# The last pair of row tiles gets an order of its own: column halves in two banks, residual and norm weights early, row factors on two engines

## The chip, the cores and the metric

The kernel runs on one core of one Trainium2 chip. The time is device microseconds (us) of that core for one execution of the whole program. Of the kernel before, three runs are shown: 2419.07, 2419.09 and 2419.3 us, so the median is 2419.09 us. A profiled execution of the same program took 2419.82 us. Times inside a profile are counted from the start of its span.

## The reference

A layer of a bidirectional encoder in float32, for a prompt of 2048 rows and a sample of 256 rows with 1024 columns each: a mixer half (Fourier mixing and retention) and an MLP half, both with a norm and a residual, and a last norm behind it. Only the end of the layer matters here:

```python
h = modulate(rmsnorm(x, norm_mlp), sh2, sc2)
x = x + gt2[:, None, :] * (jnp.square(jax.nn.relu(h @ w_mlp_in)) @ w_mlp_out)
return rmsnorm(x, norm_final)     # x * rsqrt(mean(x * x, -1) + EPS) * norm_final
```

So every output row needs its product with `w_mlp_out` (4096 x 1024), times the gate `gt2`, plus the residual `x`, and then one factor per row (the inverse root of its mean square) and one weight per column (`norm_final`).

## The kernel before, in words

The 2304 rows stand in 18 tiles of 128 rows. The last stage, from `HB = ...` on, multiplies the squared activations by `w_mlp_out`. It takes the tiles in nine pairs: pairs 0 to 7 are the prompt, pair 8 (tiles 16 and 17) is the sample. The inner dimension is cut into four rounds (`for r in range(NG)`), each with its own weights in SBUF. In the rounds 0 to 2 the partial sums of a pair go to HBM (`accd`) and come back in the round after; in the round 3 they are finished and stored.

A pair in a round is one 2 x 2 block product: two tiles of rows, two halves of the inner dimension, two halves of 512 columns. It is done with seven products in place of eight (`STEPS`, Winograd's form); I call them product 0 to product 6. A product multiplies a left operand (`A11`, `S2`, ..., from the tile `hr`) by a right operand (`B11`, `T2`, ..., held as `wo...`). Both are held as a high and a low part, so a product is three passes (high by high, high by low, low by high) over four slices of the inner dimension: 12 matmuls with 512 columns that add up in one PSUM bank. The left operand is the one loaded as weights; ScalarE (ACT) rounds it to its high part (a CAST at L80) and VectorE (DVE) subtracts to get the low part (L81), into a tile `ho`.

The products 0, 2, 4 and 6 share the bank X: product 2 is added on top of what product 0 left there, and so on. Products 3 and 5 share Z, product 1 has Y. After every product DVE adds the bank to one of the four blocks of the accumulator `acc` (L1201; `ADDR` gives the block: 0, 0, 1, 3, 3, 1, 2). Blocks 0 and 1 are the column halves of the pair's first tile, 2 and 3 those of the second. Product 2 may write X only when DVE has read what product 0 left, and so on up to product 6.

In round 3 a tile is done after product 5 (first tile) or product 6 (second). `finish_tile` (L1134 to L1138) handles 1024 columns at once: DVE multiplies by the gate and adds the residual `x1`, ACT squares and sums the row (L145), GpSimd (POOL) scales, adds EPS (L102) and raises to -0.5 (L105), DVE multiplies by the row factor `rr` and the norm weights `nf` (L1137), and SyncE (SP) issues the store. For the last pair `finish_block` (L1143 to L1146) does gate, residual and square by blocks of 512 columns, as soon as a block is whole, and `finish_rows` (L1148 to L1155) adds the two sums (DVE), forms the factor (POOL) and scales and stores both halves (DVE, SP).

The gate of the sample differs from that of the prompt. It is loaded just ahead of pair 8 (L888) into a slot of the pool `rawb`, where it has to wait until the gate of the prompt has had its last reader, L1134 of tile 15. The residual tiles `x1` rotate through the five slots of the pool `raw`.

The program is written in the order of the loops. A scheduler then sets the order on each engine, and every engine works through its own queue in that order. SP's queue holds all the loads and stores of the stage, so a load that waits there holds up those behind it.

Of the kernel before, what the change touches and what calls it, by code (L numbers as in the profile page):

```python
# [15 lines left out]
P = 128  # L16
# [15 lines left out]
def encoder(ctx: ExitStack, tc: tile.TileContext, a):  # L32
# [1110 lines left out]
    def finish_block(b, y, x1, ss):  # L1143
        dve.tensor_tensor(out=y, in0=y, in1=gate[:, halves(b)], op=ALU.mult)
        dve.tensor_tensor(out=y, in0=y, in1=x1[:, halves(b)], op=ALU.add)
        act.activation(x1[:, halves(b)], y, AF.Square, accum_out=ss[:, b % 2:b % 2 + 1])  # L1146

    def finish_rows(t, y, ss):  # L1148
        dve.tensor_tensor(out=ss[:, 2:3], in0=ss[:, 0:1], in1=ss[:, 1:2], op=ALU.add)
        r = rstd_from(ss[:, 2:3], 1, 1.0 / D)  # L1150
        for b in range(2):
            yb = y[:, 512 * b:512 * b + 512]
            dve.scalar_tensor_tensor(out=yb, in0=yb, scalar=r[:, 0:1], in1=nf[:, halves(b)],
                                     op0=ALU.mult, op1=ALU.mult)
            sp.dma_start(out=xrows("y", t)[:, halves(b)], in_=yb)  # L1155

    for r in range(NG):
        w = load_mo(r)
        if r == NG - 1:
            gate = load_gate(1, 0, lambda s: v1(s, "rawb"))  # L1160
            nf = v1("nf", "rawb")
            sp.dma_start(out=nf, in_=a["norm_final"].rearrange("(o c) -> o c", o=1).to_broadcast([P, D]))
        for pr in range(NT // 2):
            if r == NG - 1 and pr == NP // 2:
                gate = load_gate(1, 1, lambda s: v1(s, "rawb"))
            c, pc = divmod(pr, NPC)
            hv = v1("hr", f"hr{pr % 2}").rearrange("p (j b s) -> p j b s", j=GJ, b=7)
            sp.dma_start(out=hv[:, :, 0:NB[r], :].rearrange("p j b s -> p j (b s)"),
# [12 lines left out]
            if r == NG - 1:  # L1181
                x1 = [v1("x1", "raw") for _ in range(2)]
                for i in range(2):
                    sp.dma_start(out=x1[i], in_=x1d[2 * pr + i])
            at = {}
            ss = [tsm([P, 4], "ss") for _ in range(2)] if end else None
            for i, (ln, rn, bn) in enumerate(STEPS):
                ho = v1("ho", f"ho{nho[0] // 3 % 2}", F32R)
                nho[0] += 1
                hh, hl = ho[:, 0:512], ho[:, 512:1024]  # L1190
                split(src[ln], hh.rearrange("p (j s) -> p j s", j=GJ), hl.rearrange("p (j s) -> p j s", j=GJ))
                if i in (0, 1, 3):
                    at[bn] = bank(bn)
                o = at[bn]
                three(lambda p_, j, first, last: add_mm(
                    i, o, (hh, hh, hl)[p_][:, j * P:(j + 1) * P], w[j][rn][p_ % 2], first, last), range(GJ))
                b_ = ADDR[i]
                if r == 0 and i in (0, 2, 3, 6):
                    act.copy(acc[:, b_], o)
                else:  # L1200
                    dve.tensor_tensor(out=acc[:, b_], in0=o, in1=acc[:, b_], op=ALU.add)  # L1201
                if end:
                    if i not in (0, 2, 3):
                        finish_block(b_, acc[:, b_], x1[b_ // 2], ss[b_ // 2])
                    if i > 4:
                        finish_rows(2 * pr + b_ // 2, rows[b_ // 2], ss[b_ // 2])
                elif r == NG - 1 and i > 4:
# [78 lines left out]
```

## Time and profile before

| | |
|---|---|
| median of three runs | 2419.09 us |
| profiled execution, the run / its span | 2419.82 / 2417.9 us |
| PE (TensorE matmul) busy | 2349.4 us, 97% of the span, 11985 matmuls |
| DVE / ACT / POOL busy | 1465.5 / 1004.8 / 112.0 us |
| mean granted TensorE clock | 0.989 of full speed |
| product 6 of pair 8, the last one | starts at 2405.89 us, 12 matmuls, 3.00 us |
| last store issued | 2414.7 us |

Reading it: a row of the timeline has the start in us, the busy time in us, the engine, the line of the kernel, the operation, the tile written and the tile read, the shape and the count; in square brackets stands how long the engine had been idle before and what released it. Rows of one line that follow each other are merged. A row of the waits names who waited for whom, the total, the number of times and the longest. SPq is SyncE's queue, which issues DMAs. In the table of stages each row has the length of the stage, the busy time of PE, the weight loads (PEld), DVE, ACT and POOL, the granted clock and the DMA share.

### The profile page before, as it was taken

What the parts mean: (1) busy time and instruction counts of PE and PEld (TensorE: products, weight loads), DVE (VectorE), ACT (ScalarE), POOL (GpSimd) and SP (SyncE); (2) the same over time, 40 slices, a digit from 0 to 9 for tenths busy, and PEclk for the clock granted to TensorE, in tenths of its full rate; (3) what the DMA queues carried; (4) which work ended last, traced back from release to release, by engine and by line L of the source; (5) the groups of instructions that cost most, each with busy time, mean ns of one, the idle gap of its engine ahead of it and who ended that gap; (6) DMA issues with size and microseconds to landing.
All of it is one profiled execution on the core that took longest, in us unless ns stands there. A gap on an engine that the chain in (4) does not pass through costs nothing.

```text
span 2417.9 us, 30874 instructions
## 1 busy us (share of the span) xinstructions
PE 2349.4 (97%) x11985; PEld 2040.2 (84%) x11985; DVE 1465.5 (61%) x2188; ACT 1004.8 (42%) x1684; POOL 112.0 (5%) x191
## 2 busy tenths in 40 slices
PE   7999999999999999999999999999899999999998
PEld 4777787788887888999999999998688788787886
DVE  3574544334544754655685578556646867857788
ACT  4742222123333533555565566555334323224332
POOL 0101000001111000000000000000000000000000
PEclk9999999999999999999999999999899999999999
DMA  7547649323333455543453345443534645545774
GB/s 284 210 154 270 208 152 330 136 75 134 126 101 107 157 166 170 182 136 122 159 186 122 122 159 183 130 134 124 180 118 140 217 157 192 192 157 221 269 265 163
DMA packets 183770, 411.61 MB, mean 170 GB/s; under 512 B 12052, under 2 KB 80436, under 8 KB 176712
## 3 DMA queue, kind: packets, MB, share of 16 engines
q1 hardware_dynamic: 182040, 405.58, 48.7%
q0 software_dynamic: 1584, 4.06, 0.6%
q8 instruction: 94, 1.54, 0.3%
q14 instruction: 52, 0.43, 0.1%
HBM read 274.05 MB, written 135.54 MB: 169 GB/s over the span
## 4 chain that ended last, share of the span: by engine, by line
PE 82%; issue 8%; DVE 5%; DMA 2%; ACT 2%; POOL 1%; SPq 0%; POOLq 0%; DVEq 0%; ACTq 0%
PE mX L968 30%; PE proj L84 21%; PE mZ L968 15%; PE mY L968 7%; PE o L84 2%; PE ada L84 1%; PE dft L84 1%; PE tr L750 1%; DVE woT L81 1%; PE kvf L84 1%; DVE woB L81 1%; PE sc L84 1%; PE kvb L84 1%; POOL rr L105 1%; DVE acc L1201 1%
## 5 line engine op out<-in xcount | busy, mean ns | idle before, releaser
L968 PE MATMUL mX<-woT,ho 128*128 128x512 f32 x1296 | 312.3, 390 | 3.8 <-ACT x L1146 1.5
L80 ACT CAST ho<-hr 128x512 fp32r<-128x512 f32 x252 | 153.0, 621 | 345.3 <-PE mX L968 213.9
L968 PEld LDWEIGHTS mX<-woT,ho 128*128 128x128 f32 x1296 | 243.8, 188 | 56.5 <-issue 1.9
L968 PE MATMUL mX<-opS,wT 128*128 128x384 f32 x1152 | 208.0, 334 | 0.0
L84 PE MATMUL proj<-whi,hhi 128*128 128x512 f32 x720 | 192.0, 404 | 13.4 <-ACT hhi L80 7.8
L968 PEld LDWEIGHTS mX<-opS,wT 128*128 128x128 f32 x1152 | 200.4, 188 | 0.0
L81 DVE TENSOR_TENSOR ho<-hr,ho 128x512 fp32r<-128x512 f32 x252 | 170.2, 686 | 35.8 <-ACT ho L80 35.5
L84 PE MATMUL proj<-wlo,hhi 128*128 128x512 f32 x720 | 187.1, 397 | 0.0
L84 PE MATMUL proj<-whi,hlo 128*128 128x512 f32 x720 | 182.6, 392 | 0.0
L84 PEld LDWEIGHTS proj<-whi,hhi 128*128 128x128 f32 x720 | 132.2, 190 | 52.6 <-issue 10.9
L84 PEld LDWEIGHTS proj<-wlo,hhi 128*128 128x128 f32 x720 | 135.9, 191 | 32.3 <-issue 4.2
L84 PEld LDWEIGHTS proj<-whi,hlo 128*128 128x128 f32 x720 | 134.0, 188 | 30.5 <-issue 3.4
L81 DVE TENSOR_TENSOR wB<-mr,wB 128x1024 fp32r<-128x1024 f32 x72 | 87.9, 1221 | 81.6 <-ACT wB L80 81.4
L968 PE MATMUL mY<-woB,ho 128*128 128x512 f32 x432 | 112.0, 396 | 10.7 <-ACT woB L80 7.2
L1201 DVE TENSOR_TENSOR acc<-mX,acc 128x512 f32<-128x512 f32 x117 | 79.9, 687 | 65.5 <-PE mX L968 59.0
L968 PE MATMUL mX<-woB,ho 128*128 128x512 f32 x432 | 111.8, 398 | 6.0 <-ACT ho L80 5.9
L968 PE MATMUL mZ<-woT,ho 128*128 128x512 f32 x432 | 109.7, 395 | 5.9 <-ACT woT L80 5.5
L968 PE MATMUL mY<-opA,wB 128*128 128x384 f32 x576 | 106.1, 338 | 2.4 <-DVE x L159 2.4
L968 PEld LDWEIGHTS mY<-woB,ho 128*128 128x128 f32 x432 | 81.8, 191 | 30.0 <-ACT woB L80 8.4
L80 ACT CAST wB<-mr 128x1024 fp32r<-128x1024 f32 x72 | 75.3, 1046 | 75.6 <-PE mY L968 41.0
L968 PE MATMUL mX<-opA,wB 128*128 128x384 f32 x576 | 105.5, 334 | 0.7 <-ACT wB L80 0.7
L102 POOL TENSOR_SCALAR rv<-ss 128x1 f32<-128x1 f32 (+1 forms) x72 | 18.2, 253 | 1892.7 <-DVE acc L1201 1280.6
(243 smaller groups left out, 4308.0 us busy)
## 6 DMA issues: line engine op xcount, KB each, us to landing
mr<-w_mlp_in SPq DMA_DIRECT2D x96, 512.0 KB, 4.3
hidd<-hid SPq DMA_DIRECT2D x48, 768.0 KB, 4.0
hr<-hidd SPq DMA_DIRECT2D x27, 1024.0 KB, 6.4
accd<-acc SPq DMA_DIRECT2D x27, 1024.0 KB, 4.6
acc<-accd SPq DMA_DIRECT2D x27, 1024.0 KB, 5.1
ada<-ada_w SPq DMA_DIRECT2D x48, 512.0 KB, 7.3
h<-hd SPq DMA_DIRECT2D x36, 512.0 KB, 4.2
x<-x_prompt SPq DMA_DIRECT2D x32, 512.0 KB, 5.1
```

What stands on the lines that cost most here:

```text
L80: act.copy(hi, src)
L81: dve.tensor_tensor(out=lo, in0=src, in1=hi.bitcast(F32), op=ALU.subtract)
L84: pe.matmul(out, l, r, start=first, stop=last)
L102: pool.tensor_scalar(out=v[:, :n], in0=ss[:, :n], scalar1=scale, scalar2=EPS, op0=ALU.mult, op1=ALU.add)
L105: pool.tensor_tensor(out=r[:, :n], in0=v[:, :n], in1=mhalf[:, :n], op=ALU.pow)
L750: pe.transpose(o[:, hs], src[:, hs], ident)
L968: pe.matmul(out, l, r, start=first and fresh, stop=last, skip_group_check=not fresh)
L1201: dve.tensor_tensor(out=acc[:, b_], in0=o, in1=acc[:, b_], op=ALU.add)
```

## The change

The last pair of round 3 (pair 8) leaves the common loop and is done by a function `last_pair`. What it does:

- Products 0, 2, 4 and 6 are done in two halves of 256 columns, each in an X bank of its own: 24 matmuls of 256 columns in place of 12 of 512, and DVE reads the halves one by one.
- The left operand of a product is formed one product ahead (`left_op(i + 1)`).
- Block 2 of the accumulator is multiplied by the gate and gets the residual before any product is added to it; product 6 is multiplied by the gate on its own (into a small tile `tg`) and added.
- Gate, residual and square of blocks 0, 3 and 1 follow products 1, 4 and 5. Blocks 0 and 3 are multiplied by the norm weights at once (`gain`, into the slot of `x1`).
- The squares carry the factor 1/1024 (ACT's scale 1/32), DVE adds EPS, POOL adds two sums and takes the power.
- Of each tile's two blocks, ACT scales the one that has its norm weights already, DVE the other, and both are stored.
- The sample's gate is loaded together with the prompt's at the start of round 3, into a slot of `raw`, which it keeps to the end; `x1` rotates through the four slots left.

```diff
-            if r == NG - 1 and pr == NP // 2:
-                gate = load_gate(1, 1, lambda s: v1(s, "rawb"))
...
+            gate, gate_s = (load_gate(1, i, lambda s: v1(s, ("rawb", "raw")[i])) for i in range(2))
...
+    def last_pair(src, acc, x1, rows, w):
...
+        def gate_add(b):
+            y = acc[:, b]
+            dve.tensor_tensor(out=y, in0=y, in1=gate[:, halves(b)], op=ALU.mult)
+            add(y, y, x1[b // 2][:, halves(b)])
+
+        def square(b, k, c=full):
+            act.activation(junk[:, c], acc[:, b][:, c], AF.Square, scale=1.0 / 32,
+                           accum_out=ss[:, k:k + 1])
+
+        def gain(b):
+            dve.tensor_tensor(out=x1[b // 2][:, halves(b)], in0=acc[:, b], in1=nf[:, halves(b)], op=ALU.mult)
...
+        def rows_out(k, rest, early, late):
+            pool.tensor_tensor(out=ss[:, k:k + 1], in0=ss[:, k:k + 1], in1=ss[:, rest:rest + 1], op=ALU.add)
+            pool.tensor_tensor(out=ss[:, k:k + 1], in0=ss[:, k:k + 1], in1=mhalf[:, 0:1], op=ALU.pow)
+            r = ss[:, k:k + 1]
+            y = x1[early // 2][:, halves(early)]
+            act.activation(y, y, AF.Copy, scale=r)
+            dve.scalar_tensor_tensor(out=acc[:, late], in0=acc[:, late], scalar=r, in1=nf[:, halves(late)],
                                      op0=ALU.mult, op1=ALU.mult)
+            store(early, y)
+            store(late, acc[:, late])
+
+        left_op(0)
+        gate_add(2)
+        at = {}
+        for i, (ln, rn, bn) in enumerate(STEPS):
+            if i < 6:
+                left_op(i + 1)
+            if i in (0, 1, 3):
+                at[bn] = [(bank("X"), ha), (bank("X"), hb)] if bn == "X" else [(bank(bn), full)]
...
+            for n, (o, c) in enumerate(at[bn]):
+                oo = o[:, 0:c.stop - c.start]
+                three(lambda p_, j, first, last: add_mm(
+                    i, oo, (hh, hh, hl)[p_][:, j * P:(j + 1) * P], w[j][rn][p_ % 2][:, c], first, last), range(GJ))
+                y = acc[:, b_][:, c]
+                if i < 6:
+                    dve.tensor_tensor(out=y, in0=oo, in1=y, op=ALU.add)
+                else:
+                    t = v1("tg", "raw")[:, 0:256]
+                    dve.tensor_tensor(out=t, in0=oo, in1=gate[:, halves(b_)][:, c], op=ALU.mult)
+                    add(y, y, t)
+                    square(b_, 4 + n, c)
+            if i == 1:
+                gate_add(0)
+                square(0, 0)
+                gain(0)
...
+            elif i == 4:
+                gate_add(3)
+                square(3, 3)
+                gain(3)
+            elif i == 5:
+                gate_add(1)
+                square(1, 1)
+                rows_out(1, 6, 0, 1)
...
```

What the scheduler makes of it shows in the order on two engines. First DVE at the start of pair 8, before. `acc_19185` is the accumulator of pair 7, `acc_19330` that of pair 8; L1137 is the scaling of tile 14:

```order
L81 TENSOR_TENSOR ho_19391<-hr_19328,ho_19391 128x512
L1137 SCALAR_TENSOR_TENSOR acc_19185<-acc_19185,rr_19296,nf_18180 128x1024
L81 TENSOR_TENSOR ho_19427<-hr_19328,ho_19427 128x512
L1201 TENSOR_TENSOR acc_19330<-mX_19341,acc_19330 128x512
L1201 TENSOR_TENSOR acc_19185<-mX_19194,acc_19185 128x512
L1201 TENSOR_TENSOR acc_19330<-mY_19358,acc_19330 128x512
```

The same place now. Pair 7 has `acc_19187`, its lines have moved from L1201 to L1269; L1159 is the gate on block 2, L1199 adds a bank to the accumulator, L239 adds the residual:

```order
L81 TENSOR_TENSOR ho_19396<-hr_19328,ho_19396 128x512
L81 TENSOR_TENSOR ho_19442<-hr_19328,ho_19442 128x512
L1137 SCALAR_TENSOR_TENSOR acc_19187<-acc_19187,rr_19298,nf_18182 128x1024
L1159 TENSOR_TENSOR acc_19330<-acc_19330,gate_18180 128x512
L1199 TENSOR_TENSOR acc_19330<-mX_19346,acc_19330 128x256
L1199 TENSOR_TENSOR acc_19330<-mX_19347,acc_19330 128x256
L239 TENSOR_TENSOR acc_19330<-acc_19330,x_19333 128x512
L1199 TENSOR_TENSOR acc_19330<-mY_19377,acc_19330 128x512
L1269 TENSOR_TENSOR acc_19187<-mX_19196,acc_19187 128x512
```

The gate and the residual of block 2 have come in ahead of pair 7's last read of its X bank, and the read of product 0 has become two.

Then DVE at the very end, before: the last product's bank is read, gated, added, and after the sum over the row (L1149) two halves are scaled:

```order
L1201 TENSOR_TENSOR acc_19330<-mX_19341,acc_19330 128x512
L1144 TENSOR_TENSOR acc_19330<-acc_19330,gate_19326 128x512
L1145 TENSOR_TENSOR acc_19330<-acc_19330,x_19333 128x512
L1149 TENSOR_TENSOR ss_19337<-ss_19337 128x1
L1153 SCALAR_TENSOR_TENSOR acc_19330<-acc_19330,rr_19477,nf_18180 128x512 x2
```

Now, from the read of product 4's first half on. `mX_19346` and `mX_19347` are the two banks of X; L1202 takes product 6 times the gate, L1167 is `gain`, L1178 scales one block of each tile:

```order
L1199 TENSOR_TENSOR acc_19330<-mX_19346,acc_19330 128x256
L239 TENSOR_TENSOR acc_19330<-acc_19330,x_19332 128x512
L1199 TENSOR_TENSOR acc_19330<-mX_19347,acc_19330 128x256
L1159 TENSOR_TENSOR acc_19330<-acc_19330,gate_18180 128x512
L1202 TENSOR_TENSOR tg_19512<-mX_19346,gate_18180 128x256
L239 TENSOR_TENSOR acc_19330<-acc_19330,x_19333 128x512
L239 TENSOR_TENSOR acc_19330<-acc_19330,tg_19512 128x256
L1167 TENSOR_TENSOR x_19333<-acc_19330,nf_18182 128x512
L1202 TENSOR_TENSOR tg_19528<-mX_19347,gate_18180 128x256
L239 TENSOR_TENSOR acc_19330<-acc_19330,tg_19528 128x256
L1219 TENSOR_SCALAR sl_19336<-sl_19336 128x1
L1178 SCALAR_TENSOR_TENSOR acc_19330<-acc_19330,sl_19336,nf_18182 128x512 x2
```

Behind the last product two instructions of 256 columns are left per half; gate and residual of blocks 1 and 3 and the `gain` of block 3 stand between the two halves.

Last SP's queue, before. `x_19332` and `x_19333` are the residual tiles of pair 8, the first `y_prompt` here is tile 12, the next tile 13:

```order
L1178 DMA acc_19185<-accd_14357 128x2048
L1184 DMA x_19333<-x1d_8013 128x1024
L1138 DMA y_prompt<-acc_19042 128x1024 x2
L1178 DMA acc_19330<-accd_14358 128x2048
L1138 DMA y_prompt<-acc_19185 128x1024
L888 DMA gate_19326<-gates_121 128x1024
L1138 DMA y_prompt<-acc_19185 128x1024
L1155 DMA y_sample<-acc_19330 128x512 x4
```

And now:

```order
L1244 DMA acc_19187<-accd_14357 128x2048
L1250 DMA x_19332<-x1d_8011 128x1024
L1138 DMA y_prompt<-acc_19044 128x1024
L1250 DMA x_19333<-x1d_8013 128x1024
L1138 DMA y_prompt<-acc_19044 128x1024
L1244 DMA acc_19330<-accd_14358 128x2048
L1138 DMA y_prompt<-acc_19187 128x1024 x2
L1170 DMA y_sample<-x_19332 128x512
L1170 DMA y_sample<-acc_19330 128x512
L1170 DMA y_sample<-x_19333 128x512
L1170 DMA y_sample<-acc_19330 128x512
```

The gate's load is gone from here, and every residual tile is loaded one place later: the second one of pair 8 now stands right ahead of the store of tile 13 and so ahead of the load of pair 8's partial sums, which waits for that store.

More of the change, by code (lines that the diff above doesn't have):

```diff
@@ L1141, in halves, with left_op, store @@
         return slice(b % 2 * 512, b % 2 * 512 + 512)
[L1143 to L1153, printed above, removed]
-                                     op0=ALU.mult, op1=ALU.mult)
-            sp.dma_start(out=xrows("y", t)[:, halves(b)], in_=yb)
+    def last_pair(src, acc, x1, rows, w):
+        full, ha, hb = slice(0, 512), slice(0, 256), slice(256, 512)
+        ss = tsm([P, 8], "sl")
+        ho = {}
+        junk = v1("tj", "raw")
+        def left_op(i):
+            t = v1("ho", f"ho{nho[0] // 3 % 2}", F32R)
+            nho[0] += 1
+            ho[i] = t[:, 0:512], t[:, 512:1024]
+            split(src[STEPS[i][0]], *(x.rearrange("p (j s) -> p j s", j=GJ) for x in ho[i]))
+        def gate_add(b):
[7 more added lines that the diff above has]
+            dve.tensor_tensor(out=x1[b // 2][:, halves(b)], in0=acc[:, b], in1=nf[:, halves(b)], op=ALU.mult)
+        def store(b, y):
+            sp.dma_start(out=xrows("y", NT - 2 + b // 2)[:, halves(b)], in_=y)
+        def rows_out(k, rest, early, late):
[5 more added lines that the diff above has]
+            dve.scalar_tensor_tensor(out=acc[:, late], in0=acc[:, late], scalar=r, in1=nf[:, halves(late)],
+                                     op0=ALU.mult, op1=ALU.mult)
+            store(early, y)
[8 more added lines that the diff above has]
+                at[bn] = [(bank("X"), ha), (bank("X"), hb)] if bn == "X" else [(bank(bn), full)]
+            hh, hl = ho[i]
+            b_ = ADDR[i]
+            for n, (o, c) in enumerate(at[bn]):
[14 more added lines that the diff above has]
+                gain(0)
+                dve.tensor_scalar(out=ss[:, 6:7], in0=ss[:, 0:1], scalar1=EPS, scalar2=None, op0=ALU.add)
+            elif i == 4:
[6 more added lines that the diff above has]
+                rows_out(1, 6, 0, 1)
+            elif i == 6:
+                dve.tensor_scalar(out=ss[:, 7:8], in0=ss[:, 3:4], scalar1=ss[:, 4:5], scalar2=EPS,
+                                  op0=ALU.add, op1=ALU.add)
+                rows_out(5, 7, 3, 2)
@@ L1164, in encoder @@
             if r == NG - 1 and pr == NP // 2:
-                gate = load_gate(1, 1, lambda s: v1(s, "rawb"))
+                gate = gate_s
             c, pc = divmod(pr, NPC)
@@ L1184, in encoder @@
                     sp.dma_start(out=x1[i], in_=x1d[2 * pr + i])
+            if end:
+                last_pair(src, acc, x1, rows, w)
+                break
             at = {}
-            ss = [tsm([P, 4], "ss") for _ in range(2)] if end else None
             for i, (ln, rn, bn) in enumerate(STEPS):
@@ L1201, in encoder @@
                     dve.tensor_tensor(out=acc[:, b_], in0=o, in1=acc[:, b_], op=ALU.add)
[L1202 to L1207, printed above, removed]
+                if r == NG - 1 and i > 4:
                     finish_tile(2 * pr + b_ // 2, rows[b_ // 2], x1[b_ // 2])
```

1 line of the change is left out of this document (removed).

## The prediction

> **What bounds the kernel now.** I read the page first, then the waits of PE in the last stage, the table of stages of the last 28 us, the timeline of the end, and last the DMA issues of the last two pairs.
>
> ```profile
> span 2417.9 us, 30874 instructions
> ...
> PE 2349.4 (97%) x11985; PEld 2040.2 (84%) x11985; DVE 1465.5 (61%) x2188; ACT 1004.8 (42%) x1684; POOL 112.0 (5%) x191
> ```
>
> ```profile
> PE mX L968 <- ACT x L1146: 1.5, 1, 1.5
> ```
>
> PE is busy for 97% of the span. The second row is the whole list of PE's waits from 2240 us to the end: there is one, of 1.5 us. So nothing in round 3 before pair 8 can be shortened by this change; it can win that one wait and what lies behind the last matmul. The stages:
>
> ```profile
> core 0: us, PE busy (x) PEld busy (x) DVE busy (x) ACT busy (x) POOL busy (x), PEclk, DMA share, GB/s
> 2390.00:2400.00 10.00, 10.00 (x46) 8.26 (x45) 8.78 (x12) 2.90 (x6) 0.95 (x4) 1.00 0.53 198
> 2400.00:2405.00 5.00, 4.36 (x20) 3.27 (x18) 4.42 (x6) 0.72 (x2) 0.53 (x1) 1.00 0.21 87
> ```
>
> The averages hide that DVE is nearly as full as PE here: 8.78 of 10 us, then 4.42 of 5. The wait itself, in the timeline:
>
> ```profile
> 2398.76 2.88 PE L968 MATMUL mZ<-woB,ho 128*128 128x512 f32 x12
> ...
> 2400.47 0.69 DVE L1144 TENSOR_TENSOR acc<-acc,gate 128x512 f32<-128x512 f32 x1 [0.82 <-DMA gate<-gates]
> ...
> 2401.48 2.88 PE L968 MATMUL mX<-woT,ho 128*128 128x512 f32 x12
> 2401.81 1.28 DVE L1137 SCALAR_TENSOR_TENSOR acc<-acc,rr,nf 128x1024 f32<-128x1024 f32 x1
> ...
> 2403.01 0.68 DVE L1201 TENSOR_TENSOR acc<-mZ,acc 128x512 f32<-128x512 f32 x1
> ...
> 2404.45 0.69 DVE L1145 TENSOR_TENSOR acc<-acc,x 128x512 f32<-128x512 f32 x1
> 2405.06 0.68 DVE L1201 TENSOR_TENSOR acc<-mX,acc 128x512 f32<-128x512 f32 x1
> ...
> 2405.89 3.00 PE L968 MATMUL mX<-woT,ho 128*128 128x512 f32 x12 [1.53 <-ACT x L1146]
> ```
>
> PE is through with product 4 at 2401.48 + 2.88 = 2404.36. Product 6 adds to the same bank, so it needs DVE's read of product 4 (L1201, 2405.06 to 2405.74), and starts at 2405.89. The waits name ACT, but it is this read. DVE is late because it stood 0.82 us for the sample's gate and then had tile 15 in hand. The end:
>
> ```profile
> 2408.70 6.36 SPq L1155 DMA_DIRECT2D y_sample<-acc  x4
> 2409.25 0.68 DVE L1201 TENSOR_TENSOR acc<-mX,acc 128x512 f32<-128x512 f32 x1
> 2409.97 0.69 DVE L1144 TENSOR_TENSOR acc<-acc,gate 128x512 f32<-128x512 f32 x1
> 2410.70 0.69 DVE L1145 TENSOR_TENSOR acc<-acc,x 128x512 f32<-128x512 f32 x1
> 2411.42 0.63 ACT L1146 ACTIVATE x<-acc 128x512 f32<-128x512 f32 x1 [3.41 <-DVE acc L1145]
> 2411.95 0.19 ACT L1146 ACTIVATION_READ_ACCUMULATOR x<-acc 128x1 f32 x1
> 2412.17 0.16 DVE L1149 TENSOR_TENSOR ss<-ss 128x1 f32<-128x1 f32 x1 [0.79 <-ACT x L1146]
> 2412.42 0.19 POOL L102 TENSOR_SCALAR rv<-ss 128x1 f32<-128x1 f32 x1 [4.54 <-DVE ss L1149]
> 2412.69 0.55 POOL L105 TENSOR_TENSOR rr<-rv,mhalf 128x1 f32<-128x1 f32 x1
> 2413.28 1.42 DVE L1153 SCALAR_TENSOR_TENSOR acc<-acc,rr,nf 128x512 f32<-128x512 f32 x2 [0.95 <-POOL rr L105]
> ```
>
> The last product ends at 2408.89. Then one instruction waits for another until the row factor is there at 2413.24 and the last of four stores is issued, at 2408.70 + 6.36 - 0.33 = 2414.73. From there to the end of the span it is 3.2 us, which stay. The profiled run took 2419.82 us, 1.9 more than its span and 0.7 more than the median of 2419.09; I sum in the span's time and take the difference off the median.
>
> **The change part by part: prices.** Starts in a row of equal instructions give PE 2.72 us for 12 matmuls (2398.76 to 2401.48), 0.227 each; DVE 0.61 for 512 columns (2404.45 to 2405.06), or 0.72 where the next needs the result (2409.25 to 2409.97); L1137 1.20 (2401.81 to 2403.01). For 256 columns I go to the matmuls of another stage (first the table of a stretch, for the tile dft alone, then its timeline) and to the groups of instructions:
>
> ```profile
> 204.60:206.40 1.80, 1.55 (x12) 1.57 (x12) 0.00 (x0) 0.52 (x1) 1.00 0.05 8
> ```
>
> ```profile
> 204.85 0.52 PE L84 MATMUL dft<-tab,zh 128*128 128x256 f32 x3
> ...
> 206.28 1.78 PE L84 MATMUL proj<-wlo,hhi 128*128 128x512 f32 x7
> ```
>
> ```profile
> L1057 DVE TENSOR_TENSOR hid<-mX,c 128x384 f32<-128x384 f32 x48 | 26.7, 556 | 39.1 <-PE mX L968 38.9
> L809 ACT ACTIVATE rT<-sg 128x128 f32<-128x128 f32 x72 | 21.4, 299 | 1.3
> L1135 DVE TENSOR_TENSOR acc<-acc,x 128x1024 f32<-128x1024 f32 x16 | 19.5, 1221 | 0.3
> ```
>
> Twelve matmuls of 256 columns, each with its own weight load, go by in 206.28 - 204.85 = 1.43 us, 0.12 each. DVE with 256 columns is in no row: 384 take 0.556 and 512 take 0.69, so 0.42 on that line, 0.34 to the next start (starts come 0.08 before ends). ACT's square: 0.41 between 0.299 (128) and 0.63 (512); with the read of the sum 0.72 for 512 and 0.50 for 256. A DVE row of 1024 is 1.22, 1.14 to the next start. POOL's add of two sums has no row; between its 0.19 and 0.55 I take 0.19, that of the other simple operation.
>
> Here the Trainium skill speaks against the halves. TensorE: Matmul & The Clock Gate says (LDWEIGHTS) that a load takes its columns over 1.2 GHz, so 107 ns for 128, and (Part 3, what overlaps and what doesn't) that a load overlaps with matmuls in flight only when the row group differs. By that, 48 more full loads would be an estimated 5.1 us more on PE, and in place of the 2417.6 below it would be about 2422.7 us. The trace does not agree: 0.12 us for a load and its matmul together leave no room for it.
>
> *Matmuls by halves:* products 0, 2, 4 and 6 take 24 x 0.12 = 2.88 in place of 2.72, so 0.16 more each, all on PE's path: 0.64.
>
> *Left operands one ahead, the gate early:* the operands cost the same instructions as before, off the path. The gate's 0.82 wait goes, and with it the load between two stores in SP's queue. It is paid by one load more at the start of round 3, where PE waits nowhere, and by residual tiles one place later in SP's queue. That is harmless for the residuals, which are read a pair later, but not for what stands behind them:
>
> ```profile
> 2364.59 0.32 SPq L1184 DMA_DIRECT2D x<-x1d  x1
> 2367.03 0.34 SPq L1138 DMA_DIRECT2D y_prompt<-acc  x1
> 2370.63 0.32 SPq L1178 DMA_DIRECT2D acc<-accd  x1
> ```
>
> ```profile
> DMA to landing us min/median/max: 4.7/5.1/7.9
> ```
>
> ```profile
> 2384.23 2.66 PE L968 MATMUL mX<-woB,ho 128*128 128x512 f32 x11
> ```
>
> ```profile
> 2381.68 1.06 ACT L145 ACTIVATE x<-acc 128x1024 f32<-128x1024 f32 x1 [3.88 <-DVE acc L1135]
> ...
> 2385.29 0.34 SPq L1138 DMA_DIRECT2D y_prompt<-acc  x1
> ...
> 2387.96 0.33 SPq L1178 DMA_DIRECT2D acc<-accd  x1
> ...
> 2391.24 1.28 DVE L1137 SCALAR_TENSOR_TENSOR acc<-acc,rr,nf 128x1024 f32<-128x1024 f32 x1
> ...
> 2393.04 1.28 DVE L1201 TENSOR_TENSOR acc<-mX,acc 128x512 f32<-128x512 f32 x2
> ```
>
> The load of pair 8's sums waits until the store of tile 13 (2385.29) has landed. Before, it is issued 2.67 behind it. In pair 7, where a residual load stands right ahead of the store, it is 3.60 (2367.03 to 2370.63). Now pair 8 has that too (its slot comes free with the square at 2381.68), so I put the issue at 2388.9 and, with 4.7 to land, the sums at 2393.6, some 0.6 to 0.9 later than before.
>
> *Block 2 gated first:* L1159 is now the first on DVE to need those sums, and in front of pair 7's last read. DVE is ready for it by 2391.24 + 0.61 + 1.20 = 2393.05, with both splits ahead of L1137, so it waits to 2393.6. From there DVE has no pause: L1159, two halves of product 0, residual, product 1: 0.61 + 0.34 + 0.34 + 0.61 + 0.61 = 2.5, to 2396.1 (PE has pair 7's last product ready by then: from 2384.23 on, where product 0 begins, it has 11 and 13 matmuls of 256 columns and three times 12 of 512 ahead of it: 24 x 0.12 + 36 x 0.227 = 11.05 make 2395.3, and 0.16 until the last has ended). Then pair 7's read, a gate, the last split, L1134, product 3, a residual, the first half of product 2, L1135, its second half, a gain and EPS: 6 x 0.61 + 2 x 1.14 + 2 x 0.34 + 0.1 = 6.7, to 2402.8. Product 5's read 0.72, a gate 0.61, L1137 1.20: 2405.4. The first half of product 4 is read by 2405.8. PE could have begun product 6 at 2404.36 + 3 x 0.16 = 2404.84, but waits for it: 2405.83, about as before.
>
> *The last product by halves:* its halves end at 2405.83 + 11 x 0.12 + 0.28 = 2407.4 and, 1.44 later, 2408.9. DVE has a residual, a half read and a gate until 2407.4, takes the first half (0.34), then block 3's residual (to 2408.5), the first add, the gain, and is through with the second half's two instructions at 2410.2.
>
> *The squares:* they stand in ACT's order behind block 3's residual: 512, 512, 256 and 256 columns, 0.72 + 0.72 + 0.50 + 0.60 and 0.1 of handovers, from 2408.6 to 2411.2. So ACT is late last, not DVE. The add over two sums and L102 are replaced by one POOL add: 0.1 + 0.19 + 0.08 + 0.55 gives the factor at 2412.1, 1.1 earlier than 2413.24.
>
> *Factors on two engines:* before, the last store is issued 2414.73 - 2413.24 = 1.5 behind the factor; now ACT needs 0.63 and DVE 0.75 at the same time and SP issues twice, 0.33 apart: 1.05. The last store is issued at 2413.2, 1.5 earlier than before.
>
> Sum: 2419.09 - 1.5 = 2417.6 us. A measurement here tells 0.2% (4.8 us) from no change, so this counts as the same. Bounds: with 256 columns at half of 0.61 it is 0.3 better; the sums landed at 2393.05 or earlier, 0.5 better; POOL's add at 0.55, 0.4 worse.
>
> **The rivals.**
>
> *A. Halving the columns does not halve the matmul* (slower). If a matmul of 256 columns keeps the 0.227 of 512, each of the four products takes 5.44. PE comes to product 6 at 2404.36 + 3 x 2.72 = 2412.5 and ends at 2418.1. Behind it nothing is queued: DVE 0.9, ACT 0.65, POOL 0.9, scale and stores 1.05, in all 3.5 to the last store at 2421.6, 6.9 late: 2426.0 us. It decides (4.8 us slower) from a pitch of about 0.2. By the rule of the Trainium skill on loads the pitch would be about that, 0.12 + 0.107. Against it stand the twelve matmuls at 0.12. Chance 0.03.
>
> *B. DVE's halves cost what a whole costs, 0.61.* Five of them lie before product 6 and two more before ACT's squares: 7 x 0.27 = 1.9, so 0.4 slower than before, 2419.5 us. For it: no row shows 256 columns. Against it: 384 columns cost less than 512. Chance 0.08.
>
> *C. The partial sums land late.* DVE is without a pause behind them, so each us costs one. The longest landing, 7.9, makes 2396.8, 3.2 more than forecast: 2420.8. At 1.5 us the gain is gone. For it: a residual load, two stores and the sums are now in flight together. Chance 0.08.
>
> *D. The change frees more than I sum:* DVE keeps up, product 6 starts at 2404.84, ends at 2407.9, and the 3.5 of rival A follow: 2411.4, 3.3 earlier, 2415.8 us. It needs a DVE that is a us ahead of my sum. Chance 0.05.
>
> **How the numbers follow.** The forecast has 0.76. All cases but A end within 0.2% of the time before, so the same has 0.95. Slower has 0.04: A, and 0.01 of C for a landing far beyond the longest one. Faster has 0.01, taken from D, though D as summed stays 1.5 us short of it. For the range I take the bounds of the forecast (0.8 better in all) and part of D, 2416.3, and above it B and most of C, 2419.6; outside are A and the ends of C and D.
>
> **What would show it.** Right: no wait of DVE for the gate; DVE waiting for the accumulator's load near 2393.6 and then without a pause; product 6 starting within 0.4 us of 2405.8, in two runs of 12 matmuls some 1.44 us each; four squares in a row on ACT at the end; the last store issued near 2413.2. Wrong: matmuls of 256 columns more than 0.15 apart (A), DVE rows of 256 columns at 0.6 or more (B), the accumulator's load landing behind 2395 (C), or PE beginning product 6 before 2405 (D).

## The result and the profile after

The changed kernel takes 2428.45 us, the median of 6 runs (2425.6 to 2431.79), against 2416.72 us for the kernel before in the same sessions (6 runs, 2414.0 to 2419.3). The ratio is 1.0048, 95% interval 1.0037 to 1.0059: about 11.7 us slower, well beyond the 0.2% that the prediction calls no change. Forecast were 1.5 us less. The kernel before took 2419.07 to 2419.3 us in three of its runs and 2414.0 to 2414.37 in the other three, so a gain of 1.5 us could hardly have shown in the whole time.

The profiled execution took 2429.89 us. From its page, the lines that answer to the first ones shown of before:

```profile
span 2427.8 us, 30997 instructions
...
PE 2360.7 (97%) x12033; PEld 2050.8 (84%) x12033; DVE 1467.8 (60%) x2194; ACT 1005.3 (41%) x1688; POOL 112.6 (5%) x191
```

The 48 more matmuls are there, but PE is busy 11.3 us longer, and 48 matmuls of 0.12 us are no 11 us. Where the time went is read from a table of stages whose borders are the same instructions in both kernels, found in the timelines: four matmuls `adat<-ident` in the projections, the first matmul `wo<-wohi`, the start of the long stretch of 128x384 matmuls, its end, and the first matmul of pair 8's product 0. The columns are those of the prediction's table. Before:

```profile
0.00:440.31 440.31, 419.88 (x2109) 319.11 (x2109) 221.70 (x403) 166.58 (x284) 38.92 (x67) 0.98 0.64 223
440.31:752.10 311.79, 305.24 (x1730) 262.54 (x1729) 131.02 (x254) 96.38 (x245) 37.78 (x46) 1.00 0.35 116
752.10:992.89 240.79, 234.82 (x1143) 197.56 (x1142) 140.04 (x210) 104.02 (x223) 19.96 (x42) 0.99 0.50 165
992.89:1683.56 690.67, 690.67 (x3984) 690.67 (x3985) 443.28 (x521) 390.01 (x503) 0.00 (x0) 1.00 0.44 144
1683.56:2384.23 700.67, 675.70 (x2925) 551.87 (x2925) 504.13 (x769) 240.34 (x415) 11.95 (x28) 0.98 0.53 191
2384.23:2417.90 33.67, 23.13 (x101) 18.50 (x99) 25.29 (x35) 7.47 (x16) 3.40 (x8) 0.92 0.34 125
```

After:

```profile
0.00:438.23 438.23, 418.78 (x2109) 318.62 (x2110) 221.62 (x403) 166.03 (x284) 39.21 (x67) 0.99 0.63 224
438.23:753.63 315.40, 308.85 (x1731) 262.98 (x1729) 131.39 (x254) 96.30 (x245) 38.04 (x46) 1.00 0.34 115
753.63:992.51 238.88, 231.79 (x1144) 194.57 (x1142) 139.67 (x208) 103.53 (x222) 19.96 (x42) 1.00 0.50 165
992.51:1693.78 701.27, 701.27 (x3987) 701.27 (x3986) 444.89 (x524) 389.97 (x503) 0.00 (x0) 1.00 0.44 142
1693.78:2395.48 701.70, 676.08 (x2925) 552.01 (x2925) 504.83 (x768) 240.43 (x415) 11.90 (x28) 0.98 0.53 191
2395.48:2427.80 32.32, 23.95 (x149) 21.31 (x147) 25.37 (x41) 9.09 (x20) 3.48 (x8) 0.92 0.33 123
```

The last row is the changed code, and it is faster: 32.32 us in place of 33.67, a gain of 1.35 (forecast 1.5). Everything was lost ahead of it: -2.08, +3.61, -1.91, +10.60 and +1.03 us, together 11.25. There PE, DVE and ACT have the same instructions in the same order in both kernels; only the loads of round 3, in the fifth row, are queued otherwise. The fourth row holds nearly all. There PE is busy without a gap in both kernels, with the same 3984 matmuls (the counts in the rows take in a few that overlap a border) at the same granted clock of 1.00; it only takes 10.60 us longer for them, 2.7 ns for each. The instructions that touch one operand of this stage (the tile `opA`) in a stretch of 100 us, with the shortest, median and longest duration in ns, show which instruction became longer. Before:

```profile
L968 PEld LDWEIGHTS mX<-opA,wB x96: 187/188/188, 1101.0 to 1192.3; 128*128 128x128 f32 x96
L968 PE MATMUL mX<-opA,wB x96: 334/334/334, 1101.2 to 1192.5; 128*128 128x384 f32 x96
```

After:

```profile
L968 PEld LDWEIGHTS mX<-opA,wB x96: 187/188/188, 1102.2 to 1195.0; 128*128 128x128 f32 x96
L968 PE MATMUL mX<-opA,wB x96: 336/337/343, 1102.4 to 1195.2; 128*128 128x384 f32 x96
```

The weight loads are as they were. The matmuls take 334 ns every time before, and after between 336 and 343. (They overlap, so what counts for the time is the pitch, from one start to the next: 600 us over their count, below.) The same shows in the second row of the tables, in the projections. Eight matmuls of 512 columns go from one start to the next in 484.62 - 482.80 = 1.82 us before and in 483.13 - 481.27 = 1.86 us after:

```profile
482.80 1.98 PE L84 MATMUL proj<-whi,hlo 128*128 128x512 f32 x8
484.62 1.98 PE L84 MATMUL proj<-whi,hhi 128*128 128x512 f32 x8
```

```profile
481.27 2.02 PE L84 MATMUL proj<-whi,hlo 128*128 128x512 f32 x8
483.13 2.02 PE L84 MATMUL proj<-whi,hhi 128*128 128x512 f32 x8
```

And the end of the program, the part that the prediction was about, after:

```profile
2395.90 0.34 SPq L1138 DMA_DIRECT2D y_prompt<-acc  x1
...
2398.58 0.32 SPq L1244 DMA_DIRECT2D acc<-accd  x1
...
2403.82 0.68 DVE L1159 TENSOR_TENSOR acc<-acc,gate 128x512 f32<-128x512 f32 x1
...
2407.47 3.03 PE L968 MATMUL mX<-woT,ho 128*128 128x256 f32 x24
2410.54 2.97 PE L968 MATMUL mZ<-woB,ho 128*128 128x512 f32 x12
...
2416.64 3.10 PE L968 MATMUL mX<-woT,ho 128*128 128x256 f32 x24 [0.26 <-DVE acc L1199]
2417.01 0.42 DVE L1199 TENSOR_TENSOR acc<-mX,acc 128x256 f32<-128x256 f32 x1
...
2421.86 0.75 DVE L1178 SCALAR_TENSOR_TENSOR acc<-acc,sl,nf 128x512 f32<-128x512 f32 x1
2421.95 0.72 POOL L1173 TENSOR_TENSOR sl<-sl 128x1 f32<-128x1 f32 x1
2422.74 0.55 POOL L1174 TENSOR_TENSOR sl<-sl,mhalf 128x1 f32<-128x1 f32 x1
2423.32 0.72 ACT L1177 ACTIVATE x<-x,sl 128x512 f32<-128x512 f32 x1 [0.74 <-POOL sl L1174]
2423.32 0.75 DVE L1178 SCALAR_TENSOR_TENSOR acc<-acc,sl,nf 128x512 f32<-128x512 f32 x1 [0.71 <-POOL sl L1174]
2424.46 0.42 SPq L1170 DMA_DIRECT2D y_sample<-acc  x1
```

To set these beside the times of before, 11.25 us are taken off: product 6 starts at 2405.39, the last factor is there at 2412.04, the last store is issued at 2413.21.

### The profile page after: what moved, and what is told of

Read it like the earlier page. It is cut to its first block, busy times and chain, and to the rows that moved or that the text cites. A ratio compares the mean times of both kernels' runs of the same rounds, so it can differ in the third digit from the quotient of the medians.

```text
span 2427.8 us, 30997 instructions
## 1 busy us (share of the span) xinstructions
PE 2360.7 (97%) x12033; PEld 2050.8 (84%) x12033; DVE 1467.8 (60%) x2194; ACT 1005.3 (41%) x1688; POOL 112.6 (5%) x191
## 3 DMA queue, kind: packets, MB, share of 16 engines
q8 instruction: 94, 1.54, 0.3%
## 4 chain that ended last, share of the span: by engine, by line
PE 83%; issue 8%; DVE 4%; DMA 2%; ACT 1%; POOL 1%; SPq 0%; POOLq 0%; ACTq 0%; DVEq 0%
PE mX L968 31%; PE proj L84 21%; PE mZ L968 15%; PE mY L968 8%; PE o L84 2%; PE ada L84 1%; PE dft L84 1%; PE tr L750 1%; DVE woT L81 1%; PE kvf L84 1%; DVE woB L81 1%; PE kvb L84 1%; PE sc L84 1%; DMA hr<-hidd 1%; POOL rr L105 1%
## 5 line engine op out<-in xcount | busy, mean ns | idle before, releaser
L968 PE MATMUL mX<-woT,ho 128*128 128x512 f32 (+1 forms) x1332 | 312.0, 384 | 2.6 <-DVE ho L81 1.1
L81 DVE TENSOR_TENSOR ho<-hr,ho 128x512 fp32r<-128x512 f32 x252 | 170.2, 686 | 35.7 <-ACT ho L80 35.4
L81 DVE TENSOR_TENSOR wB<-mr,wB 128x1024 fp32r<-128x1024 f32 x72 | 87.9, 1222 | 84.0 <-ACT wB L80 83.7
L968 PE MATMUL mX<-woB,ho 128*128 128x512 f32 (+1 forms) x444 | 112.1, 393 | 6.8 <-ACT ho L80 6.5
L1269 DVE TENSOR_TENSOR acc<-mX,acc 128x512 f32<-128x512 f32 x113 | 77.3, 687 | 65.7 <-PE mX L968 59.4
L968 PE MATMUL mZ<-opS,wT 128*128 128x384 f32 x576 | 105.9, 338 | 0.0
```

The source lines that it names most:

```text
L81: dve.tensor_tensor(out=lo, in0=src, in1=hi.bitcast(F32), op=ALU.subtract)
L968: pe.matmul(out, l, r, start=first and fresh, stop=last, skip_group_check=not fresh)
```

## The experiments

**What could lengthen a matmul that was not changed.** `last_pair` takes its sums from a new small tile: `ss = tsm([P, 8], "sl")`, 8 floats per partition, in a pool with four buffers, 128 bytes in all. That pool stands near the start of the left side of SBUF, so every tile on the left behind it moves up by 128 bytes. The tiles on the right side stay. In the long stretch the moving operand (`opS`, `opA`) lies on the left and the operand that is loaded as weights (`wT`, `wB`) on the right. The allocator puts `opS` at byte 20096 of a partition before and at 20224 after; `wT` is at 180096 in both. So the starts of the two differ by a multiple of 256 before, and by 128 more after. In the projections it is the same for three in five of the matmuls (`whi` on the left, `hhi` on the right); for the rest both operands are on the right. In the last stage both operands are on the left and move together, and there the table shows 700.67 and 701.70 us. I call "distance" the start of the moving operand less that of the weights, modulo 256 bytes.

Theory 1 was that the distance makes the loss. Theory 2: chance, two paces of the stream, of which any other timing may start either. Theory 3: the changed tail itself, with its longer program on PE.

**The first four: place and code apart.** The small tile added to the kernel before, where nothing uses it:

```diff
     def tsm(shape, name="sm", dt=F32):
         return sm.tile(shape, dt, tag=name, name=nm(name))
+
+    tsm([P, 8], "sl")
```

> The kernel before, with one thing added: a small tile of 8 floats per partition, with four buffers (128 bytes per partition), that nothing writes or reads. No instruction is added or moved; every tile on the left side of SBUF stands 128 bytes further, as in the kernel after. Theory 1 (addresses: the changed kernel is slower because its new small tile moves the left side's tiles by 128 bytes against the weights on the right side): 10 to 12 us slower than before, a ratio of 1.004 to 1.005, with the 128x384 matmuls of 1000 to 1600 us at a pitch of 176.0 ns instead of 173.3. Theory 2 (chance: the pitch falls into one of two states at the entry of a stretch, whatever the addresses): the ratio may be anything from 1.000 to 1.005, unlike from run to run. Theory 3 (the changed tail itself, its longer program on TensorE): no change, 0.9998 to 1.0002, pitch 173.3 ns.

Measured: ratio 1.0057, interval 1.0043 to 1.0071. The stage from 1000 to 1600 us, whose matmuls are all 128x384:

```profile
1000.00:1600.00 600.00, 600.00 (x3411) 600.00 (x3410) 385.14 (x445) 336.26 (x429) 0.00 (x0) 1.00 0.43 143
```

3411 matmuls in 600 us are 175.9 ns each, the same count as in the kernel after. The kernel before has 3463, 173.3 ns:

```profile
1000.00:1600.00 600.00, 600.00 (x3463) 600.00 (x3462) 390.96 (x451) 345.05 (x439) 0.00 (x0) 1.00 0.44 144
```

No instruction of the last pair is changed here and the whole loss is there, so theory 3 falls. Now the reverse, the changed kernel at the old addresses:

```diff
-        ss = tsm([P, 8], "sl")
+        ss = tsm([P, 16], "od")
```

> The kernel after, with its small tile taken from the slots of another small tile of 16 floats that is free by then: same instructions as after, and every address as in the kernel before. Theory 1 (addresses): the 11 us are gone and the gain of the last pair is left: 1.35 us under before, a ratio of 0.9992 to 0.9997, pitch of the 128x384 matmuls 173.3 ns. Theory 2 (chance): anything from 0.9994 to 1.005. Theory 3 (the changed tail, its longer program): 1.0045 to 1.005, as the kernel after.

Measured: 0.9997, interval 0.9988 to 1.0006 (11 runs, 2412.24 to 2418.26 us), and 3463 matmuls in the same 600 us:

```profile
1000.00:1600.00 600.00, 600.00 (x3463) 600.00 (x3462) 390.97 (x451) 345.92 (x440) 0.00 (x0) 1.00 0.44 144
```

Then the small tile larger, so that the left side moves by 256 bytes:

```diff
-        ss = tsm([P, 8], "sl")
+        ss = tsm([P, 16], "sl")
```

> The kernel after, with its small tile twice as large (16 floats, four buffers): the left side's tiles stand 256 bytes further than in the kernel before, 128 further than in the kernel after. Theory 1 with a period of 256 bytes: as with the old addresses, 0.9992 to 0.9997, pitch 173.3 ns. Theory 1 with any move off the old place costing: 1.003 to 1.006. Theory 2 (chance): anything from 0.9994 to 1.005. Theory 3 (the changed tail): 1.0045 to 1.005.

Measured: 0.9993, interval 0.9985 to 1.0002, and 3464 matmuls. And the small tile as it is, with the right side moved along:

```diff
-    pad.tile([P, 24], F32, name="pad")
+    pad.tile([P, 56], F32, name="pad")
```

> The kernel after with its small tile as it is, and the pad at the top of the right side 128 bytes larger: moving operands (left) and weights (right) of the 128x384 matmuls now both start at 256 modulo 512, where the kernel before has 128 and 384, the kernel after 256 and 384. Theory 1 if the distance between the two decides (modulo 256): 0.9992 to 0.9997, pitch 173.3 ns. Theory 1 if the moving operand's own place decides: 1.004 to 1.006, pitch 176 ns. Theory 2 (chance): anything from 0.9994 to 1.005. Theory 3 (the changed tail): 1.0045 to 1.005.

Measured: 0.9988, interval 0.9979 to 0.9997 (11 runs, 2412.03 to 2414.29 us); the stage again as before:

```profile
1000.00:1600.00 600.00, 600.00 (x3464) 600.00 (x3463) 391.41 (x452) 345.31 (x439) 0.00 (x0) 1.00 0.44 145
```

Both operands stand elsewhere than before and the speed is the old one. So it is the distance and not the place of either; and theory 2 falls too, since all 5 runs at distance 128 lie above 2426 us and all 33 of the three kernels at distance 0 below 2419. The last kernel also beats both of the given ones, the kernel before by 0.1%. That is not the last pair's gain alone: the three kernels at distance 0 have the same instructions, and their medians still differ by up to 2.7 us (2415.48, 2413.44, 2412.82), for which no cause is shown.

**The other side moved.** The same pad in the kernel before:

> The kernel before with the pad at the top of the right side 128 bytes larger: the left side's tiles stay where they are, the right side's (the weights of the 128x384 stage, the stationary operands of the projections) move by 128. Distance between moving and stationary operand modulo 256: 128, as in the kernel after, with the other side moved. If the distance decides: pitch 176.0 ns in the 128x384 stage and about +11 us. If it is the left tiles' own place that decides: 173.3 ns and no change.

Measured: 2434.37 us in one run, and the slow count:

```profile
1000.00:1600.00 600.00, 600.00 (x3411) 600.00 (x3410) 382.90 (x442) 335.41 (x429) 0.00 (x0) 1.00 0.44 143
```

The distance decides from this side too.

**Which distances.** The kernel before with an empty tile at the start of the left side, or with a larger pad on the right; N is the number of floats, 8 for 32 bytes; on the right the pad has 40 floats for 64 bytes more, 72 for 192:

```diff
     pad.tile([P, 24], F32, name="pad")
+    shim = tc.alloc_tile_pool(name="shim", bufs=1)
+    shim.tile([P, N], F32, name="shim")
```

> The kernel before, the left side's tiles 32 bytes further (an empty tile of 8 floats at the left side's start); start of the moving operand against the weights in the 128x384 stage, modulo 256: 32. Theory 1a (any distance other than a multiple of 256 costs the whole): pitch 176.0 ns, about +11 us. Theory 1b (the cost grows with the distance to 128): 173.3 to 174.2 ns, 0 to +4 us. Theory 1c (only distances within 32 bytes of 128 cost): 173.3 ns, no change.

> The same with 64 bytes (16 floats); distance 64 modulo 256. Theory 1a: pitch 176.0 ns, about +11 us. Theory 1b: 174.0 to 175.3 ns, +3 to +8 us. Theory 1c: 173.3 ns, no change.

> The same with 96 bytes (24 floats); distance 96 modulo 256. Theory 1a: 176.0 ns, about +11 us. Theory 1b: 174.7 to 176.0 ns, +5 to +11 us. Theory 1c: 173.3 to 176.0 ns, as it lies at the edge.

> The same with 192 bytes (48 floats); distance 192 modulo 256, as far from a multiple of 256 as 64 on the other side. Theory 1a: 176.0 ns, about +11 us. Theory 1b, if the cost is the same on both sides: as the run with 64 bytes to 0.3 ns. Theory 1c: 173.3 ns, no change.

> The kernel before with the pad at the top of the right side 64 bytes larger: weights 64 bytes lower, moving operands where they were, so the distance modulo 256 is 64, made from the other side than in the run with 64 bytes on the left. If the distance alone decides: 173.4 ns in the 128x384 stage and 229.2 ns for the projections of 430 to 745 us, both to 0.3. If the places themselves matter too: another pair of numbers.

> The same with 192 bytes: distance 192. If the distance alone decides, as with 192 bytes on the left: 173.4 ns and 233.0 ns, both to 0.3. If the places matter too: another pair of numbers.

> The kernel before, left side 160 bytes further: distance 160. At 32, 96 and 128 the 128x384 stage was slow (176.0 to 176.7 ns), at 0, 64 and 192 it was not. If a distance is good where it is an even multiple of 32 other than 128: slow, 176.4 to 176.8 ns, about +16 us. If the cost is one of distances up to 128 only: 173.4 ns.

> The same with 224 bytes: distance 224. If odd multiples of 32 are slow: 176.4 to 176.8 ns, about +16 us. If the cost is one of distances up to 128 only: 173.4 ns.

All of them, one execution each, which is enough for a pitch. The second column is 600 us over the count of matmuls in the stage's row; the third is the time of 16 matmuls of the projections, without a pause, from the start of the row `proj<-whi,hlo` near 480 us to the start of the second row behind it.

| distance, made by | 128x384, 1000 to 1600 us | 16 matmuls of 512 columns | the run, us |
|---|---|---|---|
| 0, the kernel before | 3463, 173.3 ns | 3.63 us | 2419.82 |
| 32, left | 3398, 176.6 ns | 3.73 us | 2435.89 |
| 64, left | 3463, 173.3 ns | 3.66 us | 2414.12 |
| 64, right | 3464, 173.2 ns | 3.66 us | 2417.08 |
| 96, left | 3398, 176.6 ns | 3.73 us | 2433.03 |
| 128, left | 3411, 175.9 ns | 3.72 us | 2427.10 |
| 128, right | 3411, 175.9 ns | 3.72 us | 2434.37 |
| 160, left | 3398, 176.6 ns | 3.75 us | 2436.89 |
| 192, left | 3464, 173.2 ns | 3.73 us | 2421.22 |
| 192, right | 3464, 173.2 ns | 3.73 us | 2418.20 |
| 224, left | 3463, 173.3 ns | 3.73 us | 2423.16 |

One of the rows behind the table, with 32 bytes on the left:

```profile
1000.00:1600.00 600.00, 600.00 (x3398) 600.00 (x3397) 382.40 (x442) 335.25 (x428) 0.00 (x0) 1.00 0.44 143
```

Each distance that was made from both sides (64, 128 and 192) gives the same pair of numbers, so the distance alone decides. None of my rules for its size held. Theory 1a (every distance but 0 costs the whole) fails at 64, 192 and 224 in the 128x384 stage, 1b (the cost grows up to 128) at 64, 1c (only near 128) at 32, and the guess about odd multiples of 32 fails at 224. What is left is a list: 0 costs nothing in either stage, and of the seven others tried, four cost 2.6 to 3.3 ns a matmul in one stage and all cost 2 to 8 ns in the other (0.03 to 0.12 us over 16). A longer matmul is not by itself the sign: with 64 bytes on the left those on `opA` last 335 to 337 ns in the stretch shown above, and the pitch is still 173.3. The runs' times go with it only roughly, since the kernel before by itself spread from 2412.7 to 2420.3 us over 27 runs.

**The parts of the tail.** Three runs undo one part each in the kernel with the larger pad. The measure is the time from the start of product 0 to the issue of the last store, 2407.18 - 2378.21 = 28.97 us in that kernel:

```profile
2376.67 0.69 DVE L81 TENSOR_TENSOR ho<-hr,ho 128x512 fp32r<-128x512 f32 x1 [0.29 <-ACT ho L80]
...
2378.21 1.48 PE L968 MATMUL mX<-woB,ho 128*128 128x256 f32 x11
...
2386.54 0.68 DVE L1159 TENSOR_TENSOR acc<-acc,gate 128x512 f32<-128x512 f32 x1
...
2405.47 0.55 POOL L1174 TENSOR_TENSOR sl<-sl,mhalf 128x1 f32<-128x1 f32 x1
...
2407.18 0.42 SPq L1170 DMA_DIRECT2D y_sample<-acc  x1
```

How much a single execution tells by this measure shows where the code of the last pair is the same. The changed kernel and the one at the old addresses take 28.98 us, but the run with 256 bytes takes 2410.49 - 2381.08 = 29.41. There DVE waits 0.44 us for the load of the sums, which is rival C of the prediction on a small scale:

```profile
2381.08 1.48 PE L968 MATMUL mX<-woB,ho 128*128 128x256 f32 x11
...
2390.31 0.69 DVE L1159 TENSOR_TENSOR acc<-acc,gate 128x512 f32<-128x512 f32 x1 [0.44 <-DMA acc<-accd]
```

With the last pair of the kernel before, the eleven profiled executions (that kernel and its ten variants with moved addresses) take 30.17 to 31.17 us. So the change as a whole gains in the last pair, as the two ranges are apart. A difference of less than 1 us between two single executions is not a cost of the edit until the trace shows where it comes from.

The products whole:

```diff
-                at[bn] = [(bank("X"), ha), (bank("X"), hb)] if bn == "X" else [(bank(bn), full)]
+                at[bn] = [(bank(bn), full)]
...
-                    t = v1("tg", "raw")[:, 0:256]
+                    t = v1("tg", "raw")[:, 0:512]
...
-                    square(b_, 4 + n, c)
+                    square(b_, 5 + n, c)
...
-                dve.tensor_scalar(out=ss[:, 7:8], in0=ss[:, 3:4], scalar1=ss[:, 4:5], scalar2=EPS,
-                                  op0=ALU.add, op1=ALU.add)
+                dve.tensor_scalar(out=ss[:, 7:8], in0=ss[:, 3:4], scalar1=EPS, scalar2=None, op0=ALU.add)
```

> The changed last pair with its operands at distance 0 (the run with the larger pad), but the four products of bank X whole, 512 columns in one bank, not in two halves. Read from the start of the pair's product 0 to the issue of the last store, 28.97 us with halves. If the halves bring the overlap of the last product's additions with its matmuls that the prediction counts: the last store comes 0.4 to 0.8 us later (29.4 to 29.8). If the four times 0.16 us that the halves cost on TensorE take back what they bring: within 0.3 us (28.7 to 29.3).

Measured: 2410.06 - 2380.09 = 29.97 us, 1.00 later, more than either expectation. PE again waits 1.22 us before product 6 for DVE's read of product 4, where the halves left a wait of 0.26 and the kernel before one of 1.53:

```profile
2380.09 2.66 PE L968 MATMUL mX<-woB,ho 128*128 128x512 f32 x11
...
2380.20 0.69 DVE L81 TENSOR_TENSOR ho<-hr,ho 128x512 fp32r<-128x512 f32 x1 [1.18 <-ACT ho L80]
...
2389.87 0.69 DVE L1159 TENSOR_TENSOR acc<-acc,gate 128x512 f32<-128x512 f32 x1
...
2402.38 3.00 PE L968 MATMUL mX<-woT,ho 128*128 128x512 f32 x12 [1.22 <-DVE acc L1199]
...
2410.06 0.42 SPq L1170 DMA_DIRECT2D y_sample<-acc  x1
```

But this run does not price the halves, because DVE was late before they could matter. Its split L81 starts 0.11 us behind product 0, and 1.54 ahead of it with the larger pad, though up to there DVE and ACT have the same instructions in the same order. L1159 starts 9.78 us behind product 0 in place of 8.33 (the scheduler has also put ACT's row sum L145 ahead of a CAST, as in the kernel before; with halves the CAST comes first). From L1159 to the last store it is 2410.06 - 2389.87 = 20.19 us with the products whole and 2407.18 - 2386.54 = 20.64 with halves. What the halves are worth stays open.

Row factors on VectorE alone:

```diff
-            y = x1[early // 2][:, halves(early)]
-            act.activation(y, y, AF.Copy, scale=r)
-            dve.scalar_tensor_tensor(out=acc[:, late], in0=acc[:, late], scalar=r, in1=nf[:, halves(late)],
-                                     op0=ALU.mult, op1=ALU.mult)
-            store(early, y)
-            store(late, acc[:, late])
+            for b in (early, late):
+                dve.scalar_tensor_tensor(out=acc[:, b], in0=acc[:, b], scalar=r, in1=nf[:, halves(b)],
+                                         op0=ALU.mult, op1=ALU.mult)
+                store(b, acc[:, b])
...
-                gain(0)
...
-                gain(3)
```

> The same with the last pair's row factors on VectorE alone, row factor and norm weights in one operation for each of the two banks, as in the kernel before, instead of one bank on ScalarE beside the other on VectorE. By the durations in the trace the second multiplication starts 0.61 to 0.75 us later, but the two stores' issues on SyncE's queue (0.38 us each) already stand in a row: the last store 0.2 to 0.4 us later (29.2 to 29.4). If the whole 0.7 shows: 29.6 to 29.8.

Measured: 29.68 us, 0.71 later, and my lower guess was wrong. Here the trace shows where it comes from. Some 0.4 of it is POOL, whose power took 0.94 us in place of 0.55. Against product 0 it began when it had begun there (2406.97 - 2379.71 = 27.26 us, as 2405.47 - 2378.21) and ended 0.39 later. It ran beside the multiplications of the pair's first tile, which now stand in a row on DVE until 2406.09 + 1.42 = 2407.51. The rest is the second multiplication in a row for the last tile.

```profile
2379.71 1.48 PE L968 MATMUL mX<-woB,ho 128*128 128x256 f32 x11
...
2406.09 1.42 DVE L1177 SCALAR_TENSOR_TENSOR acc<-acc,sl,nf 128x512 f32<-128x512 f32 x2
...
2406.97 0.94 POOL L1174 TENSOR_TENSOR sl<-sl,mhalf 128x1 f32<-128x1 f32 x1
```

Gate and residual late:

```diff
         left_op(0)
-        gate_add(2)
...
-                    t = v1("tg", "raw")[:, 0:256]
-                    dve.tensor_tensor(out=t, in0=oo, in1=gate[:, halves(b_)][:, c], op=ALU.mult)
-                    add(y, y, t)
+                    dve.tensor_tensor(out=y, in0=oo, in1=y, op=ALU.add)
+                    dve.tensor_tensor(out=y, in0=y, in1=gate[:, halves(b_)][:, c], op=ALU.mult)
+                    add(y, y, x1[b_ // 2][:, halves(b_)][:, c])
```

> The same with the gate and the residual of the last product's bank applied late, after the last partial sum, as in the kernel before: three VectorE operations of 256 columns for each half behind the last matmul instead of two. Last store 0.33 to 0.45 us later (29.3 to 29.4); if ScalarE's squares and not VectorE end last there, no change (28.9 to 29.1).

Measured: 2409.30 - 2380.12 = 29.18 us, 0.21 later, less than DVE's third operation by itself. Without the early gate DVE keeps up, and PE goes from product 4 to product 6 without a pause: 48 matmuls in one row, where the early gate left a wait of 0.26 us. PE is through 23.55 us behind product 0, against 24.25 with the early gate, and the last store follows 5.63 us later, against 4.72. That gives most of the cost back. But 0.21 us is less than the same code differs by (28.97 to 29.41), and DVE waited 0.64 us for the load of the sums in this run, so it is not settled whether the early gate gains.

```profile
2380.12 1.48 PE L968 MATMUL mX<-woB,ho 128*128 128x256 f32 x11
...
2389.21 0.81 DVE L1198 TENSOR_TENSOR acc<-mX,acc 128x256 f32<-128x256 f32 x2 [0.64 <-DMA acc<-accd]
...
2397.72 5.95 PE L968 MATMUL mX<-woT,ho 128*128 128x256 f32 x48
...
2409.30 0.45 SPq L1170 DMA_DIRECT2D y_sample<-acc  x1
```

Of the three parts only the row factors on two engines are shown to gain by themselves; the halves and the early gate are not. None of them explains a loss of 11 us.

## Why the prediction was wrong

- **The step that failed** is the sum, "2419.09 - 1.5 = 2417.6 us". It takes the 2384 us ahead of the last pair as they were: all that it counts there is one load more and the residual tiles one place later, at no cost. The runs showed 11.25 us more in them, 10.60 of these in the 128x384 stage. The prediction priced operations, queues and loads, but not memory: the new tile of 128 bytes is in no term, and none of the rivals A to D is about it. Without the move of addresses (the changed kernel at the old ones) the ratio is 0.9997, interval 0.9988 to 1.0006, in which the forecast of 0.9994 lies, and no change at all lies too.
- **The range and the chance** failed with it: "the same", meant as within 0.2%, had 0.95 because every case was one of the last 30 us.
- **"Nothing in round 3 before pair 8 can be shortened"** held; that it can be lengthened without any wait was not considered. A list of waits shows no such loss, as PE is busy throughout: 690.67 of 690.67 us before, 701.27 of 701.27 after.
- **Matmuls by halves** were right in size. 24 matmuls of 256 columns go by in 2410.54 - 2407.47 = 3.07 us against 2.88 forecast (and in 2394.98 - 2392.10 = 2.88 in the run with the late gate), far from the 5.44 of rival A; so the rule of the Trainium skill (TensorE: Matmul & The Clock Gate, Part 3) that a load overlaps only when the row group differs does not describe these rows.
- **The load of the sums** was wrong by 1.6 us to the safe side. It is issued 2398.58 - 2395.90 = 2.68 us behind the store of tile 13, not 3.60, and DVE did not wait for it: L1159 starts at 2403.82, 2392.57 on the clock of before, where 2393.6 was forecast. That was in part luck: in two of the runs above DVE did wait for this load, 0.44 and 0.64 us.
- **Product 6** starts at 2405.39 on that clock (forecast 2405.83), 0.5 earlier than before. Halves cost DVE 0.42 us, as estimated, so rival B is out.
- **The factor and the stores**: 2412.04 (forecast 2412.1) and 2413.21 (forecast 2413.2). These agree, but not term by term: POOL's second add took 0.72 us, not 0.19, and the 0.44 by which product 6 came earlier than forecast paid for most of it. So the agreement is luck. The add began beside DVE's scaling of the pair's first tile (L1178, 2421.86 to 2422.61) and ended 0.06 us behind it, at 2422.67; the prediction counted nothing for that.
- **What is not settled**: why the distance matters. The Trainium skill (TensorE: Matmul & The Clock Gate, Part 2, Step-by-step) says that PE reads the moving operand and the weights by two independent ports, so that loading the next weights takes nothing from the running matmul. By that, a change of distance would change nothing. The traces do not agree: with loads of 188 ns beside them in both kernels, the pitch of the matmuls is 173.3 ns at distance 0 and 175.9 at 128. A conflict between the two reads would fit, but it is only argued. That loads and matmuls overlap in time is shown; that they conflict is not.

## What to carry to other kernels

A new tile is a change to every address behind it: before forecasting, compare where the operands of the hottest loop start, not only what is queued. Here the moving operand and the weights should start a multiple of 256 bytes apart; the other distances tried cost up to 3% of a stage that PE bounds, and a pad of the right size gives that back. When a kernel is slower and no wait has grown, compare the time per instruction in an unchanged stage that is full.

## What was not expected of the hardware

- A stream of matmuls in which nothing waits runs at a pitch that depends on the distance of its two operands in SBUF: 173.3 ns for 384 columns at distance 0, 64, 192 and 224, 175.9 at 128, 176.6 at 32, 96 and 160. It holds for as long as the stream does (some 690 us here), at a granted clock of 1.00.
- The slow stream is uneven: in the rows shown, the matmuls' durations lie between 336 and 343 ns at distance 128, and at distance 0 all are 334 ns.
- The kernel's pad of 96 bytes on the right is part of this. Without it the distance would be -96, that is 160 modulo 256, a slow one in both stages by the table above (not tried by itself).
- POOL's operations on one column took 0.19 to 0.72 us for an add and 0.55 to 0.94 us for a power, depending on what ran beside them. In the last pair the long ones began beside a DVE operation on tiles in SBUF and ended just behind it: the add of 0.72 us 0.06 behind (2422.67 and 2422.61), the power of 0.94 us 0.40 behind (2407.91 and 2407.51). A factor formed there is late by that much.
